# A two-layer trunk on one core: 128 copies of each bias row, made by DRAM-to-DRAM DMAs on the SP queue during layer 0 in place of four DMAs on the ACT queue

## The chip, the core and the metric

The kernel runs on one core of a Trainium2 chip. The metric is the device time of one execution in microseconds (us). The core has the engines PE (matmul), DVE (VectorE), ACT (ScalarE), POOL (GpSimd) and SP (SyncE, which only issues DMAs here), each with an instruction queue of its own that is worked off in order. DMAs are issued from the SP queue and from the ACT queue and are carried out by sixteen DMA engines. An instruction that issues a DMA stands in its engine's queue like any other.

## The reference

A trunk of two layers over a sequence of 1024 tokens with 1024 channels. Layer 0 is a retention layer with four heads, layer 1 a differential attention layer with sixteen heads and a learned bias by relative position. Each layer has one input projection, which also gives a gate, and an output projection, with norms before and after.

```python
def diff_attn_mixer(h, w_in, w_out, lq1, lk1, lq2, lk2, subln_g, rel_bias, lambda_init):
    ...
    table = rel_bias.astype(jnp.float32)          # 32 buckets x 16 heads
    def block(args):
        qblk, start = args
        logits = jnp.einsum('bhmqd,bhmkd->bhmqk', qblk, k)
        bias = table[t5_bucket(q_pos, k_pos)].transpose(2, 0, 1)
        logits = logits + bias[None, :, None]
        logits = jnp.where(mask, logits, -jnp.inf)
        probs = jax.nn.softmax(logits, axis=-1)
        attn = probs[:, :, 0] - lam * probs[:, :, 1]
    ...

for i in range(DEPTH):                            # x <- x + RMSNorm(mixer(RMSNorm(x)))
    h = rmsnorm(x, pre_norm_g[i])
    y = retention_mixer(h, ...) if i == 0 else diff_attn_mixer(h, ...)
    x = x + rmsnorm(y, post_norm_g[i])
```

## The kernel before

All products are in two parts: each operand is split into a high part (cast to float32r by ACT) and a low part (the rest, by DVE or POOL), and three matmuls stand for one product.

**Start of layer 0.** `retention_layer` loads the eight token blocks of x (L249), takes the sum of squares on ACT (L253), makes the normalised row `hn` on DVE (L259), and turns it with four transposes into a PSUM tile `ps_t`, twice a block (`norm_turn`, L148). The tiles of the two halves have one buffer each. ACT casts `ps_t` into the high part of RA (L151), DVE subtracts for the low part (L152). Between the transposes PE works on the first value projection (`proj_tstat`, L168 to L170), whose first two matmuls of a step read the high part of RA and the third the low part.

**The bias rows.** `bias_rows`, traced within that start, makes one row of 384 numbers for each of the sixteen heads (`brow`, sixteen partitions, L195): the bias by distance, and a large negative number where a key lies ahead of its query. Layer 1 needs each row shifted by one more element on each of 128 partitions. So the row is written 128 times to DRAM (`xd`, 16 x 128 x 384), and `load_bias` (L711) reads it back with a row step of 383 instead of 384, one 128 x 256 tile a head. The writing is done by four DMAs from the ACT queue (L197), each of four heads:

```python
        for i in range(0, DH, 4):
            nc.scalar.dma_start(self.xd[i:i + 4], brow[i:i + 4, :].unsqueeze(1).broadcast_to([4, P, 384]))
```

**Rest of layer 0.** For each of the four heads: projections of q, k and v, the retention itself, and the gates. `load_w` brings a weight tile of 512 KB: a load on SP into `w_raw` (two buffers, L79), a cast by ACT (L82) and a subtraction by POOL (L83), which frees the buffer. A head has four tiles of gate weights, loaded in two pairs (`wg0`), and each gate's result goes to DRAM with a DMA on the ACT queue (L426). At the second pair of the last head `lead` starts to load output weights (`load_out`, L91).

**What sets the order.** A scheduler orders the instructions of each engine when the program is built, by priorities and a simulated clock; each engine then works in that order. DMAs signal completion on eight lanes (semaphores) that SP and ACT take in turn, and a DMA waits until the DMA that had its lane before it has landed.

Of the kernel before, what the change touches and what calls it, by code (L numbers as in the profile page):

```python
# [10 lines left out]
F32 = mybir.dt.float32  # L11
# [8 lines left out]
P = 128  # L20
# [7 lines left out]
DH = 16  # L28
# [18 lines left out]
def _f32(ap):  # L47
    return ap.bitcast(F32)


class _Trunk:
# [24 lines left out]
    def load_w(self, src):  # L76
        nc = self.nc
        raw = self.wp.tile([P, 1024], F32, tag="raw", name="w_raw", bufs=2)
        nc.sync.dma_start(raw, src)  # L79
        h = self.wp.tile([P, 1024], F32R, tag="wh", name="w_h", bufs=3)  # L80
        l = self.wp.tile([P, 1024], F32R, tag="wl", name="w_l", bufs=3)
        nc.scalar.copy(h, raw)  # L82
        nc.gpsimd.tensor_sub(l, raw, _f32(h))  # L83
        return h, l
# [87 lines left out]
    def bias_rows(self, pool, psm):  # L172
        nc, io = self.nc, self.io
        lv = pool.tile([P, 4, 64], F32, name="lv")
        nc.sync.dma_start(lv, io["lam"].rearrange("a d -> (a d)").unsqueeze(0).broadcast_to([P, 256]).rearrange("p (a d) -> p a d", a=4))
        lp = pool.tile([P, 2, 64], F32, name="lp")
        nc.vector.tensor_mul(lp, lv[:, 0:2, :], lv[:, 2:4, :])
        ls = pool.tile([P, 2], F32, name="ls")
        nc.vector.tensor_reduce(out=ls, in_=lp, axis=AX.X, op=ALU.add)
        le = pool.tile([P, 2], F32, name="le")  # L180
        nc.scalar.activation(le, ls, AF.Exp)
        nc.vector.scalar_tensor_tensor(self.neglam, le[:, 1:2], LAMBDA_INIT, le[:, 0:1], op0=ALU.subtract, op1=ALU.subtract)
        sub = pool.tile([P, 1], F32, name="sub_in")
        nc.sync.dma_start(sub, io["sub_g"])
        nc.vector.tensor_scalar(self.subg, sub, 0.5 * (1.0 - LAMBDA_INIT), None, op0=ALU.mult)
        onehot = pool.tile([32, 384], F32, name="onehot")
        nc.sync.dma_start(onehot, io["onehot"])
        tab = pool.tile([32, DH], F32, name="tab")
        nc.sync.dma_start(tab, io["rel_bias"])
        mrow = pool.tile([DH, 384], F32, name="mrow")  # L190
        nc.sync.dma_start(mrow, io["mrow"])
        bps = psm.tile([P, 512], F32, tag="sc", name="ps_b")
        nc.tensor.matmul(bps[0:DH, 0:384], tab, onehot, start=True, stop=True)
        brow = pool.tile([DH, 384], F32, name="brow")
        nc.vector.tensor_add(brow, bps[0:DH, 0:384], mrow)  # L195
        for i in range(0, DH, 4):
            nc.scalar.dma_start(self.xd[i:i + 4], brow[i:i + 4, :].unsqueeze(1).broadcast_to([4, P, 384]))  # L197

    def l1_qk(self, HR, QR, psm, h, order=((0, 0), (0, 1), (1, 0), (1, 1)), ws=None):
        nc, io = self.nc, self.io  # L200
# [29 lines left out]
                nc.scalar.copy(b[L], ps[U])  # L230
            yield 0.65

    # ---------------------------------------------------------------- layer 0
    def retention_layer(self, RA, RB, manual, pmm, lead):
        nc, io = self.nc, self.io
        with ExitStack() as es:
# [83 lines left out]
            def v_proj(h):  # L320
                for g in range(2):
                    ws = ws0 if h + g == 0 else [self.load_w(io["wv0"][h * 2 + g, kh]) for kh in range(2)]
                    for c in range(NCH):
                        ps = bank([P, 2, 256])
                        for t in range(2):
                            self.proj_tstat(ps[:, t, :], ws, RA, 2 * c + t)
                        hi = RB[:, 8 + 2 * c:10 + 2 * c, g * 256:g * 256 + 256]
                        lo = RB[:, 8 + 2 * c:10 + 2 * c, 512 + g * 256:512 + g * 256 + 256]
                        nc.scalar.copy(hi, ps)
                        nc.vector.tensor_sub(lo, ps, _f32(hi))  # L330
# [97 lines left out]
            for h in range(RH):  # L428
                if h == 0:
                    v_proj(h)  # L430
                    qk_proj(h)
                else:
                    qk_proj(h)
                    v_proj(h)
                ys = retention(h)
                for e0 in range(0, 4, 2):
                    ws = [self.load_w(io["wg0"][h * 4 + e0 + e]) for e in range(2)]
                    for i, (hf, e) in enumerate(((0, 0), (0, 1), (1, 0), (1, 1))):
                        if h == RH - 1 and e0 == 2:
                            lead(i)  # L440
                        gate(h, e0 + e, hf, ws[e], ys)
            manual.enter_context(self.tc.manual_schedule(engines={mybir.EngineType.PE}))
            lead(NCH)

    # ---------------------------------------------------------------- output projection, post-norm, residual
    def output_stage(self, layer, slots, nextR, prologue, head):
        nc, io = self.nc, self.io
        gsrc = self.g0 if layer == 0 else self.g1
# [115 lines left out]
                prologue()  # L564
                self.norm_turn(prev.pop(TB - 1), nextR, TB - 1, ptr, (("T", 2),) * 2)

    # ---------------------------------------------------------------- layer 1
    def attention_layer(self, HR, QR, pmm, ws0, slots):
        nc, io = self.nc, self.io
        with ExitStack() as es:  # L570
# [338 lines left out]
    def run(self):  # L909
        nc, ctx = self.nc, self.ctx  # L910
        keep = self.pool(ctx, "keep")
        self.small = self.pool(ctx, "small")
        self.wp = self.pool(ctx, "wp")
        self.dr = self.pool(ctx, "dram", DRAM)
        self.ident = keep.tile([P, P], F32, name="ident")
        make_identity(nc, self.ident)
        self.identr = keep.tile([P, P], F32R, name="identr")
        nc.vector.tensor_copy(self.identr, self.ident)
        onesf = keep.tile([P, 1], F32, name="onesf")
        nc.vector.memset(onesf, 1.0)  # L920
        self.ones = keep.tile([P, P], F32R, name="ones")
        nc.vector.tensor_copy(self.ones, onesf.broadcast_to([P, P]))
        RA = keep.tile([P, 16, 1024], F32R, name="RA")
        RB = keep.tile([P, 16, 1024], F32R, name="RB")
        self.g0 = self.dr.tile([TB, P, NE, P], F32, name="g0")
        self.g1 = self.dr.tile([TB, P, NE, P], F32, name="g1")
        self.x1d = self.dr.tile([T, D], F32, name="x1d")
        self.sgd = self.dr.tile([TB, P, DH - LATE, P], F32, name="sgd")
        self.ssd = [self.dr.tile([TB, n, P], F32, name="ssd%d" % n) for n in (BSPLIT, DH - BSPLIT)]
        self.rsd = [self.dr.tile([TB, n, P], F32, name="rsd%d" % n) for n in (BSPLIT, DH - BSPLIT)]  # L930
        a, b = (lambda i: RA[:, i, :]), (lambda i: RB[:, i, :])
        self.neglam = keep.tile([P, 1], F32, name="neglam")
        self.subg = keep.tile([P, 1], F32, name="subg")
        self.xd = self.dr.tile([DH, P, 384], F32, name="xd")
        pmm = self.pool(ctx, "pmm", PSUM)
        slots0 = [[(b(t), b(8 + t)) for t in range(8)], [(a(t), a(8 + t)) for t in range(8)]]
        heads0, tiles0 = [], []

        def lead(step):
            if step < NCH:  # L940
                for t in (2 * step, 2 * step + 1):
                    self.load_out(0, slots0, 0, t)
                if step == 0:
                    tiles0.append(self.gated8(0, ((0, 0, 8),)))
            else:
                tiles0.append(self.gated8(0, ((1, 0, 8),)))
                for tb in range(2):
                    heads0.append(pmm.tile([P, 512], F32, tag="mm", name="ps_mm", bufs=2))
                    for _ in self.out_mm(heads0[tb], tiles0[tb], slots0[0], 0, 8):
                        pass  # L950

        with ExitStack() as manual:
            self.retention_layer(RA, RB, manual, pmm, lead)
            ws0 = {}

            def prologue():
                for _ in self.l1_qk(RB, RA, pmm, 0, ((0, 0), (1, 0)), ws0):
                    pass

            early = [a(i) for i in (0, 1, 2, 3, 4, 12, 13, 14)] + [b(i) for i in range(8)]  # L960
            rest = [b(i) for i in range(8, 16)] + [a(i) for i in (5, 6, 7, 8, 9, 10, 11, 15)]
            pairs = [[(r[2 * t], r[2 * t + 1]) for t in range(8)] for r in (early, rest)]
            self.output_stage(0, slots0, RB, prologue, heads0)
            heads = self.attention_layer(RB, RA, pmm, ws0, pairs)
            self.output_stage(1, pairs, None, None, heads)
# [77 lines left out]
```

## Time and profile before

| | us |
|---|---|
| median of 3 runs | 2280.67 (2280.31 to 2282.28) |
| span of the profiled execution, first to last instruction | 2283.4 |
| PE busy | 2151.4 (94%) |
| DVE busy | 1325.8 (58%) |
| ACT busy | 852.8 (37%) |
| POOL busy | 468.3 (21%) |

The profile shows one execution, by its span; it gives no other time for it. Issuing a DMA is not counted as busy, so ACT's 37% holds no issue time. Granted clock 1.00 is TensorE's full clock.

### The profile page before, as it was taken

How to read it: one execution, taken by the hardware profiler on the slowest of the kernel's cores; microseconds unless marked ns; L12 is line 12 of the kernel's file. 1: busy time of each engine (PE TensorE's matmuls, PEld its weight loads, DVE VectorE, ACT ScalarE, POOL GpSimd, SP SyncE). 2: the span in 40 equal slices, each digit the busy share in tenths (PEclk: the TensorE clock that was granted, in tenths of full speed). 3: DMA queues.
4: the chain of work that ended last, by engine and by line, in shares of the span. 5: the costliest groups of instructions: out<-in, count | busy, mean ns of one | idle time of the engine just before them, and what ended most of it. 6: DMA issues, size and time to landing. Idle time of an engine off the chain costs nothing. (4 is left out here: it accounts for less than half of the span.)

```text
span 2283.4 us, 31018 instructions
## 1 busy us (share of the span) xinstructions
PE 2151.4 (94%) x11860; PEld 1802.3 (79%) x11860; DVE 1325.8 (58%) x3158; ACT 852.8 (37%) x1648; POOL 468.3 (21%) x260
## 2 busy tenths in 40 slices
PE   3299999999999999999999999999999999988897
PEld 2288898898898788887888888888787878876675
DVE  3225434434434645845776666676766776775766
ACT  2122122122122233334555455554545555542321
POOL 1033151151151110011111111111111011123641
PEclk7699999999999999999999999999999999999998
DMA  4220210210211454511111111111111111145874
GB/s 147 39 76 26 74 54 23 74 51 27 74 47 47 129 176 166 174 52 42 40 47 40 47 40 42 45 36 49 38 38 49 32 48 46 43 133 191 267 244 161
DMA packets 95156, 181.26 MB, mean 79 GB/s; under 512 B 8176, under 2 KB 50336, under 8 KB 94880
## 3 DMA queue, kind: packets, MB, share of 16 engines
q1 hardware_dynamic: 58064, 159.16, 21.3%
q10 hardware_dynamic: 36944, 20.13, 3.6%
q8 instruction: 93, 1.52, 0.3%
q14 instruction: 55, 0.45, 0.1%
HBM read 148.72 MB, written 30.54 MB: 79 GB/s over the span
## 5 line engine op out<-in xcount | busy, mean ns | idle before, releaser
L83 POOL TENSOR_TENSOR w_l<-w_raw,w_h 128x1024 fp32r<-128x1024 f32 x112 | 271.9, 2432 | 1402.3 <-ACT w_h L82 1395.5
L757 ACT ACTIVATE e<-ps_s,nm 128x896 f32<-128x896 f32 (+7 forms) x256 | 189.8, 742 | 104.1 <-DVE nm L755 94.0
L168 PE MATMUL ps_mm<-w_h,RA 128*128 128x256 f32 x512 | 146.0, 287 | 69.6 <-ACT RA L151 69.5
L212 PE MATMUL ps_mm<-RB,w_h 128*128 128x512 f32 x512 | 209.8, 410 | 0.3 <-ACT RB L151 0.3
L159 PE MATMUL ps_mm<-RA,w_h 128*128 128x512 f32 x512 | 205.0, 400 | 0.0
L158 PE MATMUL ps_mm<-RA,w_h 128*128 128x512 f32 x512 | 203.1, 397 | 1.6 <-DVE sg L423 1.6
L213 PE MATMUL ps_mm<-RB,w_h 128*128 128x512 f32 x512 | 202.6, 396 | 1.0 <-DVE RB L152 1.0
L214 PE MATMUL ps_mm<-RB,w_l 128*128 128x512 f32 x512 | 203.1, 397 | 0.0
L160 PE MATMUL ps_mm<-RA,w_l 128*128 128x512 f32 x512 | 202.6, 396 | 0.0
L784 ACT CAST ath<-ps_t 128x512 fp32r<-128x512 f32 (+1 forms) x192 | 91.8, 478 | 218.7 <-PE ps_t L781 212.4
L752 DVE TENSOR_REDUCE mx<-ps_s 128x1 f32<-128x640 f32 (+2 forms) x192 | 119.3, 621 | 82.5 <-PE ps_s L727 77.8
L82 ACT CAST w_h<-w_raw 128x1024 fp32r<-128x1024 f32 x112 | 117.6, 1050 | 123.4 <-PE ps_mm L159 38.7
L168 PEld LDWEIGHTS ps_mm<-w_h,RA 128*128 128x128 f32 x512 | 98.7, 193 | 70.8 <-ACT RA L151 70.4
L643 PE MATMUL ps_mm<-w_h,RB 128*128 128x256 f32 x512 | 147.6, 288 | 0.0
L170 PE MATMUL ps_mm<-w_h,RA 128*128 128x256 f32 x512 | 146.5, 287 | 0.0
L169 PE MATMUL ps_mm<-w_l,RA 128*128 128x256 f32 x512 | 145.6, 286 | 0.2 <-POOL w_l L83 0.2
L645 PE MATMUL ps_mm<-w_h,RB 128*128 128x256 f32 x512 | 143.8, 281 | 0.0
L644 PE MATMUL ps_mm<-w_l,RB 128*128 128x256 f32 x512 | 143.8, 281 | 0.0
L111 ACT CAST g_h<-w_raw 128x1024 fp32r<-128x1024 f32 x50 | 52.4, 1049 | 179.6 <-POOL w_raw L108 78.0
L158 PEld LDWEIGHTS ps_mm<-RA,w_h 128*128 128x128 f32 x512 | 96.2, 188 | 25.3 <-DVE sg L423 2.3
L214 PEld LDWEIGHTS ps_mm<-RB,w_l 128*128 128x128 f32 x512 | 96.6, 189 | 23.7
L112 DVE TENSOR_TENSOR g_l<-w_raw,g_h 128x1024 fp32r<-128x1024 f32 x50 | 70.9, 1419 | 73.5 <-ACT g_h L111 71.7
(217 smaller groups left out, 5522.2 us busy)
## 6 DMA issues: line engine op xcount, KB each, us to landing
w_raw<-in_wn SPq DMA_DIRECT2D x64, 512.0 KB
w_raw<-g SPq DMA_DIRECT2D x48, 512.0 KB
w_raw<-in_wv SPq DMA_DIRECT2D x32, 512.0 KB
w_raw<-in_wo SPq DMA_DIRECT2D x32, 512.0 KB
xt<-in_x SPq DMA_DIRECT2D x16, 512.0 KB
w_raw<-in_wg SPq DMA_DIRECT2D x16, 512.0 KB
g<-go ACTq DMA_DIRECT2D x32, 256.0 KB
g<-go ACTq DMA_DIRECT2D x64, 128.0 KB
```

What stands on the lines that cost most here:

```text
L83: nc.gpsimd.tensor_sub(l, raw, _f32(h))
L158: nc.tensor.matmul(ps, wh[:, k], region[:, kt, cols], start=(kt == 0), stop=False)
L159: nc.tensor.matmul(ps, wh[:, k], region[:, 8 + kt, cols], start=False, stop=False)
L160: nc.tensor.matmul(ps, wl[:, k], region[:, kt, cols], start=False, stop=(kt == KT - 1))
L168: nc.tensor.matmul(ps, region[:, kt, cols], wh[:, k], start=(kt == 0), stop=False)
L169: nc.tensor.matmul(ps, region[:, kt, cols], wl[:, k], start=False, stop=False)
L170: nc.tensor.matmul(ps, region[:, 8 + kt, cols], wh[:, k], start=False, stop=(kt == KT - 1))
L212: nc.tensor.matmul(ps, wh[:, k], HR[:, kt, tok], start=(kt == 0), stop=False)
L213: nc.tensor.matmul(ps, wh[:, k], HR[:, 8 + kt, tok], start=False, stop=False)
L214: nc.tensor.matmul(ps, wl[:, k], HR[:, kt, tok], start=False, stop=(kt == KT - 1))
L643: nc.tensor.matmul(ps[:, t, :], HR[:, kt, cols], wh[:, k], start=(kt == 0), stop=False)
L757: nc.scalar.activation(e[:, 0:n], S[:, 0:n], AF.Exp, bias=nm, accum_out=(s0 if m == 0 else s1))
```

## The change

`bias_rows` now writes the sixteen rows once to a small DRAM tile `bd` (16 x 384), with one DMA on the ACT queue. A new function `bias_spread` makes the 128 copies of one head with a DMA from DRAM to DRAM, `bd` to `xd`, on the SP queue. It is called in each head of layer 0 behind each of the two pairs of gate weights, for two heads of layer 1 at a time, and its DMAs are placed behind the last weight load that was traced. The bytes in `xd` and their readers are the same.

```diff
     def load_w(self, src):
         nc = self.nc
         raw = self.wp.tile([P, 1024], F32, tag="raw", name="w_raw", bufs=2)
-        nc.sync.dma_start(raw, src)
+        self.loaded = nc.sync.dma_start(raw, src)
@@ bias_rows
-        for i in range(0, DH, 4):
-            nc.scalar.dma_start(self.xd[i:i + 4], brow[i:i + 4, :].unsqueeze(1).broadcast_to([4, P, 384]))
+        nc.scalar.dma_start(self.bd, brow)
+
+    def bias_spread(self, heads):
+        with self.tc.issue_after(self.loaded.ins):
+            for h in heads:
+                self.nc.sync.dma_start(self.xd[h], self.bd[h:h + 1, :].broadcast_to([P, 384]))
@@ retention_layer, the gates of a head
                     ws = [self.load_w(io["wg0"][h * 4 + e0 + e]) for e in range(2)]
+                    self.bias_spread(range(4 * h + e0, 4 * h + e0 + 2))
                     for i, (hf, e) in enumerate(((0, 0), (0, 1), (1, 0), (1, 1))):
@@ run
         self.xd = self.dr.tile([DH, P, 384], F32, name="xd")
+        self.bd = self.dr.tile([DH, 384], F32, name="bd")
```

The orders of PE, DVE and POOL are the same in both programs, but for the line numbers. On ACT, at the start of layer 0, before (x2 is two in a row):

```order
L82 CAST w_h<-w_raw 128x1024
L181 ACTIVATE le<-ls 128x2
L197 DMA xd<-brow 512x1x384
L151 CAST RA<-ps_t 128x4x128
L197 DMA xd<-brow 512x1x384 x3
L151 CAST RA<-ps_t 128x4x128
L329 CAST RB<-ps_mm 128x2x256
```

and in the changed program:

```order
L82 CAST w_h<-w_raw 128x1024
L181 ACTIVATE le<-ls 128x2
L196 DMA bd<-brow 16x384
L151 CAST RA<-ps_t 128x4x128 x2
L333 CAST RB<-ps_mm 128x2x256
```

One DMA of 16 rows stands where the first of four with 512 rows each stood, and nothing stands between the two casts of RA any more.

On SP, from the last head's projections to the end of layer 0, before (`w_raw` from `in_wg` are gate weights, from `in_wo` output weights, from `g_79` gated output):

```order
L79 DMA w_raw<-in_wn 128x1024 x4
L79 DMA w_raw<-in_wv 128x1024 x4
L79 DMA w_raw<-in_wg 128x1024 x4
L91 DMA w_raw<-in_wo 128x1024 x2
L103 DMA w_raw<-g_79 128x1024
L91 DMA w_raw<-in_wo 128x1024 x6
```

and in the changed program:

```order
L79 DMA w_raw<-in_wn 128x1024 x4
L79 DMA w_raw<-in_wv 128x1024 x4
L79 DMA w_raw<-in_wg 128x1024 x2
L201 DMA xd<-bd 128x384 x2
L79 DMA w_raw<-in_wg 128x1024 x2
L201 DMA xd<-bd 128x384 x2
L91 DMA w_raw<-in_wo 128x1024 x2
L103 DMA w_raw<-g_79 128x1024
```

Two copies stand behind the second and two behind the fourth load of gate weights; the last two stand ahead of the first load of output weights. The other three heads have the same two pairs.

## Rows read from the trace of the kernel before

**Rows 1.** The page: span and PE's busy time, share and instructions.
```profile
span 2283.4 us, 31018 instructions
PE 2151.4 (94%) x11860; PEld 1802.3 (79%) x11860; DVE 1325.8 (58%) x3158; ACT 852.8 (37%) x1648; POOL 468.3 (21%) x260
```

**Rows 2.** Windows (us): length, busy us by engine, granted clock, DMA share, GB/s.
```profile
core 0: us, PE busy (x) PEld busy (x) DVE busy (x) ACT busy (x) POOL busy (x), PEclk, DMA share, GB/s
...
16.50:20.00 3.50, 2.44 (x13) 1.28 (x12) 3.36 (x10) 3.26 (x8) 0.00 (x0) 0.99 1.00 353
20.00:23.30 3.30, 3.30 (x17) 3.28 (x16) 3.30 (x10) 1.48 (x5) 2.02 (x1) 0.50 0.18 69
23.30:28.10 4.80, 3.96 (x32) 3.58 (x31) 4.66 (x18) 0.43 (x1) 0.35 (x1) 1.00 0.46 107
28.10:97.40 69.30, 0.04 (x1) 0.00 (x0) 0.27 (x3) 0.63 (x2) 0.00 (x0) 0.51 0.22 27
97.40:102.10 4.70, 4.68 (x22) 4.41 (x23) 3.76 (x5) 1.52 (x3) 0.00 (x0) 0.53 0.24 28
...
130.00:700.00 570.00, 569.51 (x3218) 491.60 (x3217) 237.76 (x522) 119.30 (x182) 168.40 (x120) 1.00 0.17 51
```

**Rows 3.** Waits, 20 to 125 us: who waited for whom, us, times, longest.
```profile
ACT RA L151 <- issue: 74.9, 2, 73.0
...
PE ps_mm L168 <- ACT RA L151: 69.3, 1, 69.3
```

**Rows 4.** Timeline of ACT: start, us, instruction; ACTq is issuing a DMA.
```profile
21.84 1.26 ACTq L197 DMA_DIRECT2D xd<-brow  x1
...
23.17 73.55 ACTq L197 DMA_DIRECT2D xd<-brow  x3
96.77 0.58 ACT L151 CAST RA<-ps_t 128x512 fp32r<-128x512 f32 x1 [73.03 <-issue]
```

**Rows 5.** Timeline of PE around the gap and behind it.
```profile
27.86 0.28 PE L170 MATMUL ps_mm<-w_h,RA 128*128 128x256 f32 x1
97.41 0.58 PE L168 MATMUL ps_mm<-w_h,RA 128*128 128x256 f32 x1 [69.27 <-ACT RA L151]
...
98.22 1.09 PE L148 MATMUL ps_t<-ident,hn 128*128 128x128 f32 x4
98.96 0.56 PE L170 MATMUL ps_mm<-w_h,RA 128*128 128x256 f32 x1
...
102.10 0.36 PE L170 MATMUL ps_mm<-w_h,RA 128*128 128x256 f32 x1
```

**Rows 6.** Timeline of DVE around the same gap.
```profile
27.01 1.28 DVE L259 SCALAR_TENSOR_TENSOR hn<-xt,xr,pre_g 128x1024 f32<-128x1024 f32 x1
28.20 0.15 DVE L74 SCALAR_TENSOR_TENSOR xr<-xt,xr 128x3 f32<-128x3 f32 x1
97.39 0.69 DVE L152 TENSOR_TENSOR RA<-ps_t,RA 128x512 fp32r<-128x512 f32 x1 [69.03 <-ACT RA L151]
```

**Rows 7.** Waits of the SP queue, 120 to 700 us.
```profile
SPq L79 <- POOL w_l L83: 499.5, 40, 33.5
SPq L79 <- DMA xd<-brow: 22.0, 1, 22.0
```

**Rows 8.** Timeline of SP at the last gate weights of layer 0.
```profile
705.53 0.33 SPq L79 DMA_DIRECT2D w_raw<-in_wg  x1
707.89 0.33 SPq L91 DMA_DIRECT2D w_raw<-in_wo  x1
```

**Rows 9.** Timeline of ACT at the first output weights.
```profile
711.69 1.05 ACT L92 CAST RB<-w_raw 128x1024 fp32r<-128x1024 f32 x1 [0.69 <-DMA w_raw<-in_wo]
715.83 0.63 ACT L397 ACTIVATE rh<-st 128x512 fp32r<-128x512 f32 x1 [3.09 <-DVE st L377]
```

**Rows 10.** Timeline of SP, one load of projection weights in head 0.
```profile
125.13 3.50 SPq L79 DMA_DIRECT2D w_raw<-in_wn  x1
```

**Rows 11.** Timeline of ACT, the cast of that load.
```profile
143.29 1.05 ACT L82 CAST w_h<-w_raw 128x1024 fp32r<-128x1024 f32 x1 [0.27 <-DMA w_raw<-in_wn]
```

**Rows 12.** Instructions on tile xd: duration ns min/median/max, first to last start.
```profile
L711 SPq DMA_DIRECT2D bt<-xd x16: 326/326/447, 978.6 to 1939.5; - x16
```

## Prediction

> **What bounds the kernel now.** First the page: the span is 2283.4 us and PE is busy for 94% of it [rows 1], so time comes off only where PE stands still or runs at the lower clock. The page's slices put most of PE's idle time in the second and third of forty, so I cut that stretch into windows next [rows 2]. From 28.1 to 97.4 us PE works 0.04 us out of 69.3, and ACT, DVE and POOL are empty with it; only the DMA engines work, at a share of 0.22 of sixteen, which is three and a half engines, moving 27 GB/s. From 130 to 700 us PE is busy for 569.5 us of 570. So the start of layer 0 holds one hole, and behind it PE has no gap to speak of.
>
> The view of waits names the hole [rows 3]: PE waited 69.3 us for one cast of ACT (RA, L151), and that cast waited 73 us for "issue", which is ACT itself and not any data. ACT's row of time shows what it was issuing [rows 4]: the first of the four copies of L197 took 1.26 us to issue, the other three 73.55 us together, from 23.17 to 96.7, and the cast of RA starts in the same instant, at 96.77. They hold ACT because each is 512 rows of 1.5 KB, fed to three and a half DMA engines: 768 KB at the 27 GB/s of the window take 29 us, and the issue of the later ones takes about as long as the transfer ahead of them. The transfers themselves are wanted far later: the first read of xd is at 978.6 us [rows 12].
>
> **What is removed.** In the changed program PE, DVE and POOL carry the same instructions in the same order; ACT loses four DMAs and gains one, and SP gains sixteen. So the old stretch can be replayed without the hold, step by step.
> - ACT: the one DMA that replaces the four sits at the place of the first. It is 16 rows, 24 KB. Its issue lies between 0.33 us (an issue on SP, rows 8) and 1.26 us (the 512 rows of the old one, rows 4); I take 0.4, but either ends by 23.1, before the transposes that the next cast reads. That cast then runs at 24.0 instead of 96.77.
> - PE: the matmul that started at 97.41 finds its operand ready and follows the one at 27.86 [rows 5], at about 28.1. The hole of 69.3 us is gone.
> - What is late next is DVE. Its half of RA (97.39 in the old trace) comes behind the normalised row hn at 27.01, which takes 1.28 us, and one small step of 0.15 [rows 6]. So it runs from 28.35 to 29.0. The four transposes of 98.22 write the PSUM tile that this step frees, so they run from 29.0 to 29.4, and the twelve matmuls that started at 98.96 from 29.4 to 30.9 at 0.12 us each, the spacing that the trace has at full clock. Four more transposes end at 31.3. The old trace has that point at 102.10 [rows 5].
> - The gain is 102.10 - 31.3 = **70.8 us**. It is the hole of 69.3, and 1.5 more, because PE took 4.7 us for 97.4 to 102.1 at a granted clock of 0.53 [rows 2], the lower of its two levels (1.2 of 2.4 GHz), to which it had fallen in the hole; at full clock this is 2.4 us of work, of which DVE's order takes back about 0.8.
>
> Ends for this term: with no wait for DVE at all, 69.3 + (4.7 - 2.4) = 71.6. At the other end the clock: it stood at 0.50 from 20 to 23.3, behind a stretch in which PE was busy for 2.44 us of 3.5, and at 1.00 behind that [rows 2]. The new program has a pause of 0.9 us at 28.1, and if the clock falls once more as at 20, the 3.3 us of that stretch do half the work: 1.65 us are lost, and the gain is 69.1.
>
> **What is added.** Sixteen copies of 192 KB from DRAM to DRAM, in pairs, two pairs in each of the four heads of layer 0, each pair right behind the second or the fourth load of gate weights. No row shows such a copy. Its price has these ends. Fast: at the 353 GB/s that the loads of x reach with all sixteen engines [rows 2], 0.56 us each, 1.1 a pair. Slow: at the 27 GB/s of the old copies [rows 2], 7.3 us each, 14.6 a pair. Between them lies the pace of one engine in the old copies, 27 / 3.5 = 7.7 GB/s, on all sixteen engines: 123 GB/s, 1.6 us each, 3.2 a pair. I take 3.2, since a copy now has 128 rows of a DRAM source, as the weight loads that reach 353 have, but rows of 1.5 KB.
>
> The Trainium skill (DMA: Bandwidth & Descriptors, section on why a DMA increments its semaphore by 16) says that the slowest dimension of a transfer sets how many engines share it, up to sixteen; by that rule the old copies, with four rows outermost, ran on four engines, which the 0.22 bears out, and the new ones with 128 run on all sixteen, so the sum would stand at the fast side.
>
> Who stands behind a pair: on SP the next weight load, and with it ACT's cast of that load. SP is no bound: it waits 499.5 us, in 40 pieces, for POOL to free a weight buffer [rows 7], and an issue is 0.33 us [rows 8], so sixteen issues are 5.3 us spread over eight places where it would wait anyway. The tight place is the last pair. The load of output weights at 707.89, 2.36 us behind the last gate load [rows 8], is cast by ACT at 711.69 after a wait of 0.69 for just this load, and ACT's next work, at 715.83, waits 3.09 us for DVE [rows 9]. So this load may come 3.1 us later for nothing. The pair goes out at about 706; at 3.2 us it holds the load up by less than that: cost 0. At 14.6 us a pair the load is 10 to 12 us late, ACT's next cast some 8, and PE, which reads it, up to 8. Each DMA also waits for the completion lane that it takes over, one of eight which SP and ACT share. Some of ACT's stores of gated output and some of SP's loads now wait on lanes of the copies, but by the old times the nearest such waiter comes 47 us behind its copy, so this costs 0 unless a pair takes 47. Cost of what is added: 0, with ends 0 and 8.
>
> A gain elsewhere? The old copies were still draining when ACT was free again: SP stood 22.0 us on one of their lanes [rows 7], and a load issued at 125.13 [rows 10] was cast only at 143.29, still 0.27 late [rows 11]. But PE was at its full clock and full there [rows 2], so this is worth 0.
>
> **The sum.** 2283.4 - 70.8 + 0 = 2212.6 us of span. The page gives that execution's span alone; the median of the runs, 2280.67, is 2.7 below it, and I carry this over: 2280.67 - 70.8 = 2209.9, in round numbers **2210**.
>
> **The rivals.**
> 1. The clock falls again behind the pause at 28.1. For it speaks the 0.50 at 20 us after a stretch with gaps; against it, that the stretch from 23.3 to 28.1 is fuller (3.96 of 4.8). It gives 2211.6. Chance 0.22.
> 2. The hold only changes its queue: the copies run at the old pace, 14.6 us a pair, and SP is held in issue as ACT was. Seven of the eight pairs still vanish in SP's long waits; the last costs 8: 2218. For it speaks that each copy still reads one row 128 times; against it, that this row lies in DRAM and not in one partition. Chance 0.08. The Trainium skill (the same page, section on issuing engines that are not separate DMA queues) would go further: all queues run on the same DMA engines, and moving a DMA to another one saves only issue time, usually little. By this rule alone almost nothing is won; the rows show the exception, an issue time of 73.55 us on the engine that everyone waits for [rows 4].
> 3. Slower than before: a copy lands on one DMA engine. At 7.7 GB/s a pair then takes 51 us, and each weight load behind it has a sixteenth of its rows in that line. Two pairs a head stand 102 us of queue against loads that SP issues 2 to 6 us behind them; PE would lose some 40 us a head, 160 in all: 2280.67 - 70.8 + 160 = 2370. It decides against the change from about 18 us a head, that is 32 us a pair. Against it speaks the 353 GB/s of loads with 128 rows. Chance 0.02.
> 4. The change doesn't do what it says, because ACT is held at that place by something else. The issue rows end in the very instant in which the cast begins, so I see no room: 0.01, at 2280.
> 5. More than the sum: later stretches profit from a freer start. PE has no gap there. 0.05, at 2207.
>
> **How the numbers follow.** The forecast has 0.62. Forecast, rival 1 and rival 5 reach from 2207 to 2213 with the 2 us by which the three runs differ; rival 2 begins at 2214. The range 2206.5 to 2216 leaves out most of rival 2, and rivals 3 and 4. About 0.2%, 4.6 us, is what a measurement of this kernel can tell from no change: faster 0.97, within it 0.01, slower 0.02.
>
> **What would show it.** Right: ACT's DMA near 21.8 lasts under 1.3 us, the next cast of RA starts near 24 us, PE's largest gap in 20 to 60 us is about 1 us, the point of old 102.10 stands near 31, and everything up to 700 us is shifted by 70 to 72. The pairs on SP have issues of about 0.33 us, and the cast of output weights (711.69 - 71 = 641) waits 1 to 4 us for its load. Wrong: issues of several us on SP, casts of weights that wait for loads behind the pairs, or PE gaps near the gates of layer 0.

## The result, and the profile after

| | us, median | runs | ratio to before, 95% interval |
|---|---|---|---|
| before | 2281.48 | 2280.31 to 2283.97 | |
| changed | 2211.73 | 2209.91 to 2214.69 | 0.9692 [0.9678, 0.9706] |

The change takes 69.75 us off the median; 70.8 were forecast. The profiled execution has a span of 2210.5 us.

The windows of the changed kernel answer to [rows 2]. Columns: length, busy us and instructions of PE, PEld, DVE, ACT, POOL, then granted clock, DMA share and GB/s.

```profile
16.50:20.00 3.50, 2.31 (x14) 1.42 (x13) 3.36 (x9) 3.38 (x7) 0.00 (x0) 1.00 0.98 339
20.00:23.30 3.30, 3.30 (x27) 2.87 (x26) 3.30 (x11) 2.36 (x6) 1.56 (x1) 1.00 0.30 116
23.30:28.10 4.80, 2.38 (x20) 2.17 (x20) 4.66 (x18) 1.50 (x3) 0.83 (x1) 0.98 0.36 110
28.10:31.20 3.10, 3.03 (x15) 2.76 (x15) 3.02 (x6) 0.50 (x1) 0.00 (x0) 0.50 0.02 5
31.20:59.20 28.00, 28.00 (x239) 27.80 (x239) 11.27 (x15) 8.91 (x15) 4.75 (x2) 1.00 0.26 83
59.20:630.00 570.80, 570.31 (x3226) 492.53 (x3225) 238.63 (x523) 119.31 (x183) 168.38 (x120) 1.00 0.18 54
```

The hole of 69.3 us is gone: from 28.1 to 630 us PE is never idle for longer than a fraction of a microsecond, sixteen copies or not. One thing returned, the lower clock, 0.50 from 28.1 to 31.2. And one wait of PE grew ahead of that stretch, before (first line) and in the changed kernel (second line):

```profile
26.29 0.66 PE L148 MATMUL ps_t<-ident,hn 128*128 128x128 f32 x4 [0.84 <-DVE RA L152]
26.77 0.66 PE L148 MATMUL ps_t<-ident,hn 128*128 128x128 f32 x4 [2.42 <-DVE RA L152]
```

From 20 to 23.3 us the clock now stood at 1.00, where it had stood at 0.50 [rows 2]. PE was done sooner and waited longer for DVE, 2.42 us in place of 0.84.

On ACT, the rows that answer to [rows 4]:

```profile
22.15 0.36 ACTq L196 DMA_DIRECT2D bd<-brow  x1
22.56 1.07 ACT L151 CAST RA<-ps_t 128x512 fp32r<-128x512 f32 x2 [0.80 <-DVE brow L195]
24.15 0.58 ACT L333 CAST RB<-ps_mm 128x512 fp32r<-128x512 f32 x1 [0.51 <-PE ps_mm L170]
```

The one DMA holds ACT for 0.36 us, and both casts of RA run back to back, the second of which had started at 96.77. On DVE and PE, the rows that answer to [rows 5, 6]:

```profile
27.48 1.28 DVE L263 SCALAR_TENSOR_TENSOR hn<-xt,xr,pre_g 128x1024 f32<-128x1024 f32 x1
28.67 0.15 DVE L74 SCALAR_TENSOR_TENSOR xr<-xt,xr 128x3 f32<-128x3 f32 x1
28.75 0.69 DVE L152 TENSOR_TENSOR RA<-ps_t,RA 128x512 fp32r<-128x512 f32 x1
```

```profile
29.58 1.09 PE L148 MATMUL ps_t<-ident,hn 128*128 128x128 f32 x4
32.26 0.60 PE L148 MATMUL ps_t<-ident,hn 128*128 128x128 f32 x4
32.62 0.36 PE L170 MATMUL ps_mm<-w_h,RA 128*128 128x256 f32 x1
```

DVE's half of RA comes behind hn, as the replay had it, and the transposes that stood at 98.22 come behind it. The next four (before: 101.67) start at 32.26, and the matmul of 102.10 at 32.62.

At the last pair of copies, first SP and then ACT, to be read against [rows 8, 9]:

```profile
635.77 0.33 SPq L79 DMA_DIRECT2D w_raw<-in_wg  x1
636.15 1.11 SPq L201 DMA_DIRECT2D xd<-bd  x2
638.13 0.33 SPq L91 DMA_DIRECT2D w_raw<-in_wo  x1
```

```profile
642.42 1.05 ACT L92 CAST RB<-w_raw 128x1024 fp32r<-128x1024 f32 x1 [1.19 <-DMA w_raw<-in_wo]
646.06 0.64 ACT L401 ACTIVATE rh<-st 128x512 fp32r<-128x512 f32 x1 [2.59 <-DVE st L381]
```

The output weights still leave 2.36 us behind the last gate weights; the cast waits 1.19 us in place of 0.69, and ACT's next wait for DVE shrinks from 3.09 to 2.59. So the half microsecond comes out of slack. The gate weights of 705.53 now go out at 635.77, 69.8 us earlier, and the first read of xd at 908.8 in place of 978.6 [rows 12], 69.8 as well.

### The profile page after: what moved, and what is told of

Read it like the earlier page. It is cut to its first block, busy times and chain, and to the rows that moved or that the text cites. A ratio compares the mean times of both kernels' runs of the same rounds, so it can differ in the third digit from the quotient of the medians.

```text
span 2210.5 us, 31034 instructions
## 1 busy us (share of the span) xinstructions
PE 2145.4 (97%) x11860; PEld 1798.2 (81%) x11860; DVE 1325.3 (60%) x3158; ACT 852.8 (39%) x1648; POOL 471.0 (21%) x260
## 5 line engine op out<-in xcount | busy, mean ns | idle before, releaser
L160 PEld LDWEIGHTS ps_mm<-RA,w_l 128*128 128x128 f32 x512 | 96.2, 188 | 22.0
## 6 DMA issues: line engine op xcount, KB each, us to landing
g<-go ACTq DMA_DIRECT2D x64, 128.0 KB
```

The costliest lines, as they stand in the source:

```text
L160: nc.tensor.matmul(ps, wl[:, k], region[:, kt, cols], start=False, stop=(kt == KT - 1))
```

## The experiments

Two jobs, each with the kernel before beside it; its medians there were 2282.44 and 2282.61. The **theory** is that ACT was held because 2048 rows went to few DMA engines, in one long line on each, and that the copies now hide behind SP's waits. The first **rival** is that the queue (ACT or SP) is what counts, the second that copies out of SBUF hold their issuer whatever their shape, and the third that the hidden copies cost something after all.

**The changed kernel again.**

> The changed kernel, timed beside the three others of this job on the same chip. Both theories below expect 2210 to 2213 us. In its trace the granted clock near 28 to 31 us is the open point: where it falls to 0.50 once more, the point that stood at 102.10 before stands near 32.5; where it stays at 1.00, near 31.

2214.36 us, ratio 0.9702 [0.9687, 0.9716], 1.4 us above the expected range. This execution kept its clock, and so the two together show what the lower clock costs here. Window 28.1 to 31.3, and PE's transposes:

```profile
28.10:31.30 3.20, 2.45 (x22) 2.27 (x21) 3.20 (x6) 0.59 (x1) 0.00 (x0) 1.00 0.02 5
```

```profile
26.41 0.66 PE L148 MATMUL ps_t<-ident,hn 128*128 128x128 f32 x4 [2.37 <-DVE RA L152]
...
29.22 0.63 PE L148 MATMUL ps_t<-ident,hn 128*128 128x128 f32 x4 [0.75 <-DVE RA L152]
...
31.10 0.60 PE L148 MATMUL ps_t<-ident,hn 128*128 128x128 f32 x4
31.45 0.36 PE L170 MATMUL ps_mm<-w_h,RA 128*128 128x256 f32 x1
```

At full clock PE waits 0.75 us for DVE, where the replay had 0.9, and the transposes of 101.67 start at 31.10; the replay had 30.9. With the clock at 0.50 they started at 32.26. Since that execution was 0.36 late already ahead of this stretch (26.77 against 26.41 for the transposes before), the lower clock cost about 0.8 us, not the 1.65 priced: PE would have waited for DVE anyway.

**No copies at all.** `bias_spread` is not called, and the tile of layer 1 reads `bd`:

```diff
-                    self.bias_spread(range(4 * h + e0, 4 * h + e0 + 2))
...
-                d = self.xd[h]
-                nc.sync.dma_start(bt, bass.AP(tensor=d.tensor, offset=d.offset + 127, ap=[[383, P], [1, 256]]))
+                d = self.bd[h:h + 1, :]
+                nc.sync.dma_start(bt, bass.AP(tensor=d.tensor, offset=d.offset + 127, ap=[[0, P], [1, 256]]))
```

> The changed kernel without the sixteen DRAM-to-DRAM copies: the tile of layer 1 reads the small bd row itself, 128 times without the shift by one element (this leaves out the shift of the bias, so the logits of layer 1 differ). Theory hidden: the copies lie behind SP's waits for POOL and cost nothing, so the time is that of the changed kernel within 0.1% (2209 to 2214), and ACT's cast of the first output weights waits about 0.7 us for its load in place of 1.2. Rival: the copies take DMA time from weight loads all over layer 0, and 5 us or more come off (2207 or less).

2215.41 us, ratio 0.9705 [0.9688, 0.9722], beside 0.9702 of the changed kernel in the same job (both medians lie above what I had expected, this one by 1.4 us): no difference that can be measured, so the copies cost nothing to within about 0.2%, the half width of these intervals. One detail of the expectation fell:

```profile
641.34 1.05 ACT L92 CAST RB<-w_raw 128x1024 fp32r<-128x1024 f32 x1 [1.18 <-DMA w_raw<-in_wo]
```

The cast waits 1.18 us with no copy ahead of the load, as against 1.19 with two. So the half microsecond above is not the copies' either; where it comes from stays open.

**One DMA of sixteen partitions.** The smallest change to the kernel before:

```diff
-        for i in range(0, DH, 4):
-            nc.scalar.dma_start(self.xd[i:i + 4], brow[i:i + 4, :].unsqueeze(1).broadcast_to([4, P, 384]))
+        nc.scalar.dma_start(self.xd, brow.unsqueeze(1).broadcast_to([DH, P, 384]))
```

> The kernel before with its four DMAs of four partitions made into one DMA of sixteen partitions, on the ACT queue at the same place, from SBUF as before: same 2048 rows, same bytes. Theory engines: ACT was held because each of four DMAs put 128 rows on each of four DMA engines behind 128 to 384 others; spread over sixteen engines the 2048 rows are 128 an engine with nothing ahead, as in the first DMA of before, whose issue took 1.26 us. ACT is then held 1.3 to 4 us and the time is 2210 to 2216. Rival source: 128 copies out of SBUF partitions on the ACT queue are what holds it, however they are split; ACT is held for 30 us or more and the time is 2240 or more.

2211.58 us, ratio 0.9693 [0.9679, 0.9708]: the whole gain, with the old queue, the old source and the old bytes. ACT, and a window in which the rows are moved:

```profile
22.05 0.70 ACTq L196 DMA_DIRECT2D xd<-brow  x1
22.80 1.08 ACT L151 CAST RA<-ps_t 128x512 fp32r<-128x512 f32 x2 [1.26 <-PE ps_t L148]
```

```profile
28.00:31.30 3.30, 3.30 (x25) 3.30 (x25) 3.30 (x6) 0.90 (x2) 0.00 (x0) 0.78 0.88 97
```

The DMA share is 0.88 of sixteen engines and not 0.22, and ACT is held for 0.70 us. This decides against the second rival, and against the first as a condition: neither SP nor DRAM as a source was needed.

The edit changes three things at once: DMA engines from four to sixteen, source partitions from four to sixteen, issues from four to one. Two runs below part engines and issues (the partitions come in the last section). Sixteen copies issued one behind the other hold SP for 10.73 us, 0.67 each, so a second issue is not held as such. Copies out of DRAM that run on one engine hold SP for 4.03 us a pair, where the same pair on sixteen takes 1.11, so few engines alone make a hold.

**The old four DMAs on SP.** The change of queue alone:

```diff
-            nc.scalar.dma_start(self.xd[i:i + 4], brow[i:i + 4, :].unsqueeze(1).broadcast_to([4, P, 384]))
+            nc.sync.dma_start(self.xd[i:i + 4], brow[i:i + 4, :].unsqueeze(1).broadcast_to([4, P, 384]))
```

> The kernel before with its four DMAs, as they were, issued from SP in place of ACT: the change of queue alone. Theory engines: the 73 us of issue go with the DMAs to SP; ACT and PE run on, but the load of w_raw<-in_wn, rope and the weights behind them leave SP only at about 97 us and land behind the rest of the old copies, while PE wants them near 71 us; some 25 to 60 of the 70 us are lost again: 2235 to 2270. Rival queue: what mattered was that the DMAs leave ACT, and SP has time enough: 2210 to 2216.

2298.31 us, ratio 1.0074 [1.0056, 1.0093]: a little slower than before, where I had expected 2235 to 2270. SP, then who waited in 18 to 200 us:

```profile
24.20 73.36 SPq L197 DMA_DIRECT2D xd<-brow  x4
97.67 29.72 SPq L79 DMA_DIRECT2D w_raw<-in_wn  x1
127.49 3.85 SPq L268 DMA_DIRECT2D rope<-in_rope  x1
```

```profile
ACT w_h L82 <- DMA w_raw<-in_wn: 95.4, 1, 95.4
...
PE ps_mm L168 <- DVE RB L330: 82.8, 1, 82.8
```

SP stands 73.36 us, where ACT stood 73.55 + 1.26 [rows 4]. My sum went wrong behind that: the weight load that follows was itself held in issue for 29.72 us. By the trace's DMA records its first rows move at 128.0 and the last of the old rows ends at 145.6, and ACT's cast comes behind both, at 147.4. So PE's hole is 82.8 us, longer than the old one.

**The new copies on ACT.** The form of the copy alone, at the old place:

```diff
-        nc.scalar.dma_start(self.bd, brow)
+        put = nc.scalar.dma_start(self.bd, brow)
+        with self.tc.issue_after(put.ins):
+            for h in range(DH):
+                nc.scalar.dma_start(self.xd[h], self.bd[h:h + 1, :].broadcast_to([P, 384]))
```

> The changed kernel with its sixteen DRAM-to-DRAM copies issued from ACT at the place of the old DMAs, between the casts of RA: the form of the copy alone, on the old queue. Theory engines: sixteen issues of 0.5 to 0.6 us are 9 us of ACT, put between casts where ACT stands still for 1.3 us at a time, and one wait of some 2 us for bd to land: a loss of 0 to 10 us against the changed kernel, 2211 to 2222. Rival queue: copies on ACT hold it as before, 2240 or more. The scheduler orders PE and DVE a little otherwise around the casts in this program.

2214.26 us, ratio 0.9700 [0.9672, 0.9727]: the whole gain once more. The copies sit between ACT's casts, three, three, three, two, three, two:

```profile
26.29 1.88 ACTq L199 DMA_DIRECT2D xd<-bd  x3
28.21 0.59 ACT L151 CAST RA<-ps_t 128x512 fp32r<-128x512 f32 x1 [1.36 <-PE ps_t L148]
28.23 1.90 ACTq L199 DMA_DIRECT2D xd<-bd  x3
30.17 0.59 ACT L151 CAST RA<-ps_t 128x512 fp32r<-128x512 f32 x1 [1.37 <-PE ps_t L148]
...
32.33 2.20 ACTq L199 DMA_DIRECT2D xd<-bd  x3
34.58 0.59 ACT L151 CAST RA<-ps_t 128x512 fp32r<-128x512 f32 x1 [2.11 <-PE ps_t L148]
```

An issue takes about 0.6 us. Each of these casts starts within 0.1 us of the end of an issue, so the issues do hold ACT a little: the cast of 34.58 comes 1.49 us behind the start of its transposes, where 0.6 to 0.7 us is usual. PE doesn't feel it. It waits 3.1 us for DVE, as in the second execution of the changed kernel, and its one new wait is 0.6 us, for POOL.

**All sixteen copies in one place.** `bias_spread(range(DH))` behind the first pair of gate weights, nothing later.

> The changed kernel with all sixteen copies behind the first pair of gate weights of head 0, none later. A pair took 2.4 us, so the sixteen are 19 us of DMA and some 9 us of issue in one place. The next gate load stands 6 us behind them and has some 12 to spare until its cast. Theory slack: it comes 3 to 10 us late, and PE, which works ahead on other tiles, loses 0 to 8: 2211 to 2220. Rival: SP or the DMA engines clog as ACT did, and 20 us or more are lost.

2216.08 us, ratio 0.9701 [0.9682, 0.9719]. SP issues for 10.73 us, and the gate load behind goes out at 103.62:

```profile
92.79 10.73 SPq L201 DMA_DIRECT2D xd<-bd  x16
103.62 11.24 SPq L79 DMA_DIRECT2D w_raw<-in_wg  x2
```

The cast of that load waits for PE and not for the load, and PE has no new wait. So spreading the copies over four heads is not what hides them; one of SP's long waits would have been enough.

**Copies on one engine.** 131 rows a copy, a number without a divisor, in a tile of 131 rows a head:

```diff
-        self.xd = self.dr.tile([DH, P, 384], F32, name="xd")
+        self.xd = self.dr.tile([DH, 131, 384], F32, name="xd")
...
-                self.nc.sync.dma_start(self.xd[h], self.bd[h:h + 1, :].broadcast_to([P, 384]))
+                self.nc.sync.dma_start(self.xd[h], self.bd[h:h + 1, :].broadcast_to([131, 384]))
```

> The changed kernel with 131 rows a copy in place of 128 (three rows nobody reads; 131 has no divisor), so that each copy should run on one DMA engine. A pair then takes 262 rows of about 0.1 us, some 25 us, where it took 2.4 in the changed kernel. Theory slack: the load behind a pair waits for its share on that engine; loads of gate weights have about 14 us to spare and come some 10 us late in each of four heads, the first output weights have 3 and come some 20 late: 30 to 60 us in all, 2240 to 2270. Rival: SP's waits for POOL (some 500 us in layer 0) cover the copies whatever they take, 2210 to 2216. That all copies stay on sixteen engines would show as 2.4 us a pair and no change.

2224.79 us, ratio 0.9756 [0.9737, 0.9774]: 10.4 us above the changed kernel of the same job, far less than 30 to 60. By the trace's DMA records a pair took 16 us, one row after the other, not 25. SP, ACT and PE's waits at the last pair:

```profile
635.18 4.03 SPq L201 DMA_DIRECT2D xd<-bd  x2
```

```profile
655.89 1.04 ACT L92 CAST RB<-w_raw 128x1024 fp32r<-128x1024 f32 x1 [15.63 <-DMA w_raw<-in_wo]
```

```profile
PE ps_sc L354 <- ACT s L362: 6.5, 1, 6.5
```

This is the only new wait of PE in layer 0. ACT's cast of the output weights stands 13.5 us later than in the changed kernel, ACT's chain behind them is late, and PE stands for 6.5 us and then has the lower clock for some microseconds (0.78 as the mean of 645 to 668 us). At the seven other pairs 16 us a pair cost PE no wait.

**The same, without a pair at the tight place.** The last pair is called behind the projections of q and k of the last head.

> The copies on one engine (131 rows, 16 us a pair, which cost 10 to 14 us), with the last pair taken from its place ahead of the first output weights and put behind the projections of q and k of the last head. Theory tight place: in that run PE had one wait, 6.5 us behind a cast of ACT that came late for the output weights, and the lower clock behind it; with the pair gone from there both vanish, and the time is 2210 to 2215, though fifteen of sixteen shares of slack are as before. Rival: the copies cost a little at each of the eight places, and the time stays at 2220 or more.

2213.74 us, ratio 0.9699 [0.9685, 0.9714]. PE's wait of 6.5 us is gone, and so are the 10 us. The tight place is shown, by taking it away. The new place of the pair is not quite free, though:

```profile
PE ps_t L423 <- DVE go L429: 3.0, 1, 3.0
```

This wait stands at 555 us, while the moved pair runs (541.6 to 559.4 by the DMA records). DVE had waited 10.4 us there for two stores of gated output (`go`), which land late: it looks as if they stand behind the pair on its engine. The seven pairs at their old places make no wait for PE.

## Why the prediction was right

- **The hold and its cause.** ACT was stopped by its own issue, because each DMA put 512 rows on four engines (three and a half busy, 0.22 of sixteen). The one DMA of sixteen partitions shows the second part best, with the one-engine copies beside the changed kernel's: same place, same rows, 0.70 us. The old DMAs on SP show the first: the hold goes where they go. One reading was too simple: the three later issues do not each take as long as the transfer ahead of them, 29 us. They took 13.29, 28.84 and 31.34.
- **The replacement on ACT**, 0.4 us: it took 0.36. The cast behind it stood at 23.0 and not at 24.0, which gained nothing, since PE waits for DVE there.
- **DVE as what is late next.** Right: 0.75 us of PE waiting for its half of RA, where the replay had 0.9. The replay ends at 30.9 for the transposes of 101.67; at full clock they stood at 31.10. The prediction's 0.9 is counted from 28.1 and leaves out two matmuls that run first. One sign was off: PE's largest gap in 20 to 60 us was to be about 1 us, and is 2.42. It is the older wait of 0.84 for DVE, which grew because the clock had not fallen at 20; the prediction had taken that stretch over from the old trace.
- **The clock**, rival 1, had a chance of 0.22, and in the profiled execution of the changed kernel it came true (0.50 from 28.1 to 31.2). There the matmul of 102.10 stands at 32.62, a gain of 69.5, where rival 1 had 69.1; in the second execution, with the clock at 1.00, it stands at 31.45, a gain of 70.65, where the forecast had 70.8. The other traces go both ways as well. From 28.1 to 31.3 the mean is 0.55 in the last experiment and 0.56 with the old DMAs on SP, and it is 0.78 from 28.0 with the one DMA, but 1.00 in five others, two of which (all copies in one place, copies on one engine) had the low clock at 20 us, like the kernel before. So this step isn't the same from run to run. The price of rival 1 was too high, 0.8 measured against 1.65, since PE had slack to lose. That the forecast of 2210 lies nearer to 2211.73 than the runs of one kernel lie to each other (4.8 us from lowest to highest) is in part luck: the medians cannot tell it from rival 1's 2211.6.
- **The price of a copy.** The bounds were 1.1 to 14.6 us a pair, and I took 3.2, the old pace of one engine on all sixteen. By the DMA records the rows of the last pair run from 2.3 to 4.7 us behind its first issue, 2.4 us, and the eight pairs took 2.2 to 3.8. That 3.2 lies among them is luck: a row took 0.065 us, so the pace behind the 3.2 was not the copies' (last section), and the engines carried weight loads in the same time. Issues took 0.48 to 0.60 us each where I had 0.33. Neither term reaches PE.
- **The tight place.** The slack of 3.1 us at the first output weights was read rightly, and so was the price of rival 2: 14.6 us a pair were to cost up to 8, and 16 us cost 6.5 of waiting and some clock, 10.4 in all. Of the eight places, this is the only one where PE waited.
- **Rival 3** was priced too high, as was my expectation for the copies on one engine: 51 us a pair there, 25 in the expectation, 16 measured. The pace of rival 3, 7.7 GB/s an engine, belongs to rows of `brow` that share a limit (last section). Its figure of 32 us a pair, from which the change would lose, does not follow from its 40 us a head at 51 us a pair: in proportion, 18 us a head are 23 us a pair. No run came near it.
- **The queue alone.** The rule of the Trainium skill that I weighed (DMA: Bandwidth & Descriptors, on issuing engines that are not separate DMA queues) says that DMAs run on the same sixteen engines whichever engine started them. The old DMAs on SP agree: by the DMA records a row took 0.222 us there and 0.224 from ACT. What it calls usually small, the issue time, is here the whole loss.
- **The span** fell by 72.9 us, 2 more than the replay. Up to the first read of xd the shift is 69.8, just under the 70 to 72 forecast for the time up to 700 us. The rest lies in layer 1 and the last stage, where no instruction changed and whose time varies: from that read to the end it is 1304.8 us before, 1301.7 here and 1303.0 in the second execution of the changed kernel, whose span fell by 71.0 (2212.4). The medians differ by 69.75.

What stays open is when the clock falls in the first 32 us; the runs show both, with the same program. PE's wait ahead of 28 us was 2.42 us where it fell and 2.37 where it did not.

## What to carry to other kernels

Look for the issue of a DMA in the row of the engine that issues it: a hold there stops everything behind it in that queue, and in this kernel it was 73 us that no busy share showed. Before a DMA is moved to another queue or cut into pieces, make its outermost dimension reach all DMA engines; that one line gave the whole gain here, while the move alone made the kernel slower. Where transfers are put behind loads, search for the one load whose reader has the least slack; seven of eight places bore 16 us a pair without a wait of PE, and the eighth had slack for about three.

## What the runs showed of the hardware that I had not expected

**Rows out of a few SBUF partitions share a limit.** The old copies read four partitions at a time and moved 27 GB/s at a share of 0.22 [rows 2]; the one DMA read sixteen and moved 97 GB/s at 0.88. That is about 7 GB/s for each busy engine both times (27 / 3.5 and 97 / 14), but it is not an engine's pace, nor SBUF's. By the trace's DMA records a row of `brow` in the kernel before took 0.07 us where it moved alone, 0.115 with two in flight and 0.22 with four. With the one DMA it took 0.065 us with up to six in flight and 0.22 with fourteen. And the 512-byte rows that the gates store out of SBUF took 0.027 us, 19 GB/s. So the rows in flight share something, and sixteen partitions gave 3.6 times what four gave. What it is, and whether four partitions on sixteen engines would gain anything, these runs don't show. The same rows out of DRAM, in a window of the changed kernel that has a pair and the weight load ahead of it:

```profile
117.50:118.50 1.00, 1.00 (x11) 1.00 (x10) 0.74 (x2) 0.85 (x1) 0.51 (x1) 1.00 0.98 356
```

This is 23 GB/s an engine, three times as much; a row of the copies took 0.065 us, with sixteen engines at work or with one.

**When an issue is held.** The second of the four old DMAs:

```profile
23.17 13.29 ACTq L197 DMA_DIRECT2D xd<-brow  x1
```

No issue was held that left at most 131 rows on an engine: the first of the old DMAs (512 rows on four engines, 1.26 us), the first copy of a pair on one engine (131 rows, 0.6 us), the one DMA (2048 on sixteen, 0.70 us), the sixteen copies in one place (2048 on sixteen, 0.67 us each). Issues that would have made it 256 or 262 were held: the one above, and the second copy of a pair on one engine, about 3.4 us (4.03 for both). The numbers of engines are taken from the rows in flight at a time. As an estimate from the DMA records, the three held issues of the kernel before ended when 204 to 218 rows an engine were still to move. This is not the whole rule: the weight load behind the old DMAs on SP, 8 rows an engine if all sixteen share its 128, was held until some 70 of the old rows an engine were left.
